# A LayerNorm's scale: computed on both halves of the partitions, spread by a matmul into PSUM

## The chip, the cores and the metric

The kernel runs on one core of one Trainium2 chip. Its engines work side by side, each with its own queue: TensorE (PE in the profile), VectorE (DVE), ScalarE (ACT), GpSimd (POOL) and SyncE (SP), which here issues the DMAs. SBUF and PSUM have 128 partitions. What counts is the device time of one execution in microseconds (us), the median of several runs.

## The reference

Two layers over 1024 tokens of 1024 channels, in float32. Each layer has a mixer (attention and short convolution, or pooling and latent attention) and a convolutional FFN, and behind each of the two stands a LayerNorm over the channels of a token:

```
def layer_norm(x, g, b):
    x32 = x.astype(jnp.float32)
    mu = jnp.mean(x32, axis=-1, keepdims=True)
    var = jnp.mean(jnp.square(x32 - mu), axis=-1, keepdims=True)
    y = (x32 - mu) * lax.rsqrt(var + LN_EPS)
    return (y * g + b)

x = layer_norm(DN_ALPHA * x + (1.0 + g_m) * y, ln_mix_g[l], ln_mix_b[l])
h = x * (1.0 + sc_f) + sh_f
y = conv_ffn(h, ffn_w_up[l], ffn_conv_w[l], ffn_w_down[l])
x = layer_norm(DN_ALPHA * x + (1.0 + g_f) * y, ln_ffn_g[l], ln_ffn_b[l])
```

The four norms of the two layers are what the change touches.

## The kernel before

Activations lie with channels on the partitions and tokens on the columns: eight tiles `r[0..7]` of 128 channels by 512 tokens hold one half of the tokens. Matrix products run in three passes over split operands (`mm3`: high by high, high by low, low by high; L289 to L291), where `split` (L267 on ScalarE, L268 on VectorE or GpSimd) makes a high and a low part.

A norm (class `Norm`) goes over one half of the tokens at a time. `gated` (L495, VectorE) adds a product from PSUM to the residual; `add` (L505, GpSimd) sums the eight tiles of `r` into `ln_acc`. `mean` multiplies that sum by a 128x128 tile of 1/1024 on TensorE (L515), so that every partition gets the mean of its column's token, subtracts it from the eight tiles on VectorE (L529; L521 in the last part), squares them on ScalarE and sums the squares into two tiles `ln_sq` (L536). `var` does the same with the squares (L545, PSUM, 128 identical rows), takes the root on ScalarE (L549) and the reciprocal on VectorE (L550) over all 512 columns, and multiplies the eight tiles of `r` by it (L556), VectorE with both operands in SBUF. For each tile ScalarE then makes the norm's output `xo` (L563), which SyncE stores, and GpSimd the next layer's input `h` (L572, named `r` where it is made in place, which then waits for `xo`), whose split into `h_f` feeds the next products.

TensorE's program order is written by hand. The code issues its matmuls in the order of the text, and `mean` and `var` are put off by `defer`: a running sum of estimated TensorE time (`spend`) says after which product `tick` issues them. TensorE executes in that order and doesn't overtake. The orders of VectorE, ScalarE, GpSimd and SyncE are set by a scheduler that simulates the program; `tc.high_priority` moves an instruction ahead of others that are ready.

`var` runs at nine places. N1 and N2: layer 0's mixer norm, first and second half of the tokens. N1 falls among the output projection's products (`oproj`, around 630 us), N2 among the first FFN products (`up`, around 684 us). N3 and N4: layer 0's FFN norm, among the last products of `dn` (1409 us) and among layer 1's first products (`lat`, 1447 us). N5 and N6 (1840 and 1893 us): layer 1's mixer norm, as N1 and N2. N7 to N9: the last norm, whose first half (N7, 2573 us) falls among the last `dn` products, while the second half goes in two parts of 256 columns (N8, 2592 us, and N9, 2599 us); in these two, GpSimd makes ten of the sixteen multiplications of L556. In the last part (`end`) the eight tiles of squares go to TensorE one by one, without being summed before.

In the FFN, `plain` multiplies by weights that are loaded and split on the way (`whi_up` on ScalarE; `wlo_up` on VectorE for the first half of the tokens, on GpSimd for the second); `activate` makes the three taps of the convolution (`cv`, L703, VectorE).

Of the kernel before, what the change touches and what calls it, by code (L numbers as in the profile page):

```python
# [10 lines left out]
F32 = mybir.dt.float32  # L11
# [3 lines left out]
AF = mybir.ActivationFunctionType  # L15
ALU = mybir.AluOpType
# [3 lines left out]
P = 128  # L20
D = 1024
# [8 lines left out]
LN_EPS = 1e-5  # L30
# [177 lines left out]
def trunk(ctx, tc, t, out):  # L208
    nc = tc.nc
    V, A, G, T = nc.vector, nc.scalar, nc.gpsimd, nc.tensor  # L210

    def pool(name, bufs=1, side="left", space=None):
        if space is not None:
            return tc.tile_pool(name=name, bufs=bufs, space=space, reuse_waits="tile")
        return tc.tile_pool(name=name, bufs=bufs, side=side, reuse_waits="tile")

    cpool = ctx.enter_context(pool("const"))
# [10 lines left out]
    def spend(us):  # L228
        clock[0] += us
# [13 lines left out]
    def load(dst, src, eng=None):  # L243
        (eng or nc.sync).dma_start(dst, src)
# [14 lines left out]
    def bank_aux(name):  # L259
        return aux[0].tile([P, HALF], F32, tag="aux", name=name)  # L260

    def half(hf):
        return slice(hf * HALF, (hf + 1) * HALF)

    def split(hi, lo, src, lo_eng="dve"):

        A.copy(hi, src)  # L267
        (V if lo_eng == "dve" else G).tensor_tensor(lo, src, hi.bitcast(F32), ALU.subtract)  # L268
# [42 lines left out]
    A.activation(cond, cT, AF.Silu)  # L311
    eps_ln = cpool.tile([P, 1], F32, name="eps_ln")
    V.memset(eps_ln, LN_EPS)
    eps_rms = cpool.tile([P, 1], F32, name="eps_rms")
    V.memset(eps_rms, RMS_EPS)

# [89 lines left out]
    class Stream:  # L406
# [12 lines left out]
        def open_norm(self, e):  # L419
            self.tmp = self.n.enter_context(pool(f"ln{e}_{self.name}", bufs=2, side="right"))  # L420
            self.ones = self.tmp.tile([P, P], F32, tag="ones", name="ones_d", bufs=1)
            V.memset(self.ones, 1.0 / D)

        def open_rows(self):

            self.rows = self.n.enter_context(pool(f"rows_{self.name}", side="right"))
            self.left = {F32: [], F32R: []}
            self.order = ["u0", "rawg", "cond", "u0", "mod_raw", "rawg", "u1", "u1"]
# [30 lines left out]
    class Norm:  # L459
# [79 lines left out]

        def var(self):  # L540
            r, f, hf = self.r, self.f, self.hf
            var = bank_aux("ln_var")[:, : self.c.stop - self.c.start]
            n = len(self.sq)
            for e in range(n):
                T.matmul(var, lhsT=self.st.ones, rhs=self.sq[e], start=e == 0, stop=e == n - 1)  # L545
            spend(1.7)
            rstd = self.tile("acc", "rstd")
            with tc.high_priority(offset=2 * AHEAD):
                A.activation(rstd, var, AF.Sqrt, bias=eps_ln)  # L549
                V.reciprocal(rstd, rstd)  # L550

            pooled = ()
            if rstd.shape[-1] < HALF:
                pooled = (3, 5) if self.end else PAIRED
            for dt in PAIRED:
                (G if dt in pooled else V).tensor_tensor(r[dt], r[dt], rstd, ALU.mult)  # L556
                xo = r[dt] if self.h is None else self.tile("xo", "xo")
                if self.end and dt in (3, 5, 6, 7):
                    (G if dt in pooled else V).tensor_scalar(
                        xo, r[dt], f[:, 0, dt : dt + 1], f[:, 1, dt : dt + 1], ALU.mult, ALU.add  # L560
                    )
                else:
                    A.activation(  # L563
                        xo, r[dt], AF.Identity, bias=f[:, 1, dt : dt + 1],
                        scale=f[:, 0, dt : dt + 1],
                    )
                if self.h is None:
                    load(self.dst[dt, :, half(hf)][:, self.c], xo)
                    continue
                load(xa_dram[hf, dt], xo)  # L570
                h32 = r[dt] if self.keep else self.tile("h32", "h32")
                G.tensor_scalar(  # L572
                    h32, r[dt], f[:, 2, dt : dt + 1], f[:, 3, dt : dt + 1], ALU.mult, ALU.add
                )
                split(self.h.t[hf][:, 0, dt], self.h.t[hf][:, 1, dt], h32)
# [757 lines left out]
    start = ExitStack()  # L1333
# [545 lines left out]
    with ExitStack() as s:  # L1879
# [32 lines left out]
        for hf in range(2):  # L1912
            c = half(hf)
            xs = h.xs(hf)
            for base, n, mi, lo in ((4, 3, 0, 0), (7, 2, 1, 3)):
                z = []
                acc = tmp.tile([P, HALF], F32, tag="zacc", name="zacc", bufs=2)
# [237 lines left out]
def build(nc, arrays):  # L2155
    t = {
        k: nc.dram_tensor(f"in_{k}", v.shape, mybir.dt.from_np(v.dtype), kind="ExternalInput").ap()
        for k, v in arrays.items()
    }
    out = nc.dram_tensor("out_xT", (KD, P, S), F32, kind="ExternalOutput").ap()  # L2160
    with tile.TileContext(nc, schedule_with_timeline_sim=True) as tc:
        trunk(tc, t, out)
# [15 lines left out]
```

## Time and profile before

| | us |
|---|---|
| runs | 2625.12, 2621.45, 2623.29 |
| median | 2623.29 |
| profiled execution | 2616.24 |
| its span | 2614.4 |
| PE, DVE, ACT, POOL busy | 2375.9, 2169.9, 1378.1, 1078.8 |

The profile shows one execution, from the first instruction to the last (the span); the 1.84 us around it belong to the run's time. In its rows `L556` is a line of the kernel, `r<-r,rstd` is output and inputs by the program's names, and `128x512` the shape, partitions by columns. A bracket at the end of a row is the time that the engine stood idle before it, and whose end released it. "PEclk" is the clock granted to TensorE, as a share of its full 2.4 GHz: 0.5 is the lower of its two levels, 1.2 GHz, and a value between is a mean over a stretch with both.

### The profile page before, as it was taken

What the parts mean: (1) busy time and instruction counts of PE and PEld (TensorE: products, weight loads), DVE (VectorE), ACT (ScalarE), POOL (GpSimd) and SP (SyncE); (2) the same over time, 40 slices, a digit from 0 to 9 for tenths busy, and PEclk for the clock granted to TensorE, in tenths of its full rate; (3) what the DMA queues carried; (4) which work ended last, traced back from release to release, by engine and by line L of the source; (5) the groups of instructions that cost most, each with busy time, mean ns of one, the idle gap of its engine ahead of it and who ended that gap; (6) DMA issues with size and microseconds to landing.
All of it is one profiled execution on the core that took longest, in us unless ns stands there. A gap on an engine that the chain in (4) does not pass through costs nothing. (4 is left out here: it accounts for less than half of the span.)

```text
span 2614.4 us, 32451 instructions
## 1 busy us (share of the span) xinstructions
PE 2375.9 (91%) x10762; PEld 1905.7 (73%) x10762; DVE 2169.9 (83%) x3495; ACT 1378.1 (53%) x2449; POOL 1078.8 (41%) x816
## 2 busy tenths in 40 slices
PE   6799997989978988998999898998989999998997
PEld 4678785877656767876787677887666888876786
DVE  7868888886898999988977868786798877788976
ACT  4558734884644344553434547675555555563434
POOL 0000003757663222324537535554675333334536
PEclk9999998999989999999999999999989999999999
DMA  6513320225434555344314331224432322244313
GB/s 249 170 42 108 97 69 17 74 77 163 133 107 159 183 172 162 104 132 151 91 55 130 93 111 39 68 80 151 138 110 93 109 84 82 93 139 140 100 48 107
DMA packets 126473, 289.44 MB, mean 111 GB/s; under 512 B 16032, under 2 KB 23712, under 8 KB 125408
## 3 DMA queue, kind: packets, MB, share of 16 engines
q1 hardware_dynamic: 125152, 283.16, 34.3%
q10 hardware_dynamic: 1152, 4.19, 0.5%
q8 instruction: 85, 1.39, 0.2%
q14 instruction: 84, 0.69, 0.1%
HBM read 234.87 MB, written 48.23 MB: 108 GB/s over the span
## 5 line engine op out<-in xcount | busy, mean ns | idle before, releaser
L703 DVE SCALAR_TENSOR_TENSOR cv<-u,taps,cv 128x512 f32<-128x512 f32 x352 | 308.4, 902 | 18.1 <-ACT cv L701 16.4
L834 POOL TENSOR_TENSOR s<-rawg 128x512 f32<-128x512 f32 (+3 forms) x60 | 78.4, 1307 | 258.8 <-DVE wlo_ups L268 87.1
L268 POOL TENSOR_TENSOR v<-v,v 128x512 fp32r<-128x512 f32 x8 | 11.9, 1492 | 416.9 <-ACT v L267 416.9
L999 DVE SCALAR_TENSOR_TENSOR r<-dn,mod,r 128x512 f32<-128x512 f32 x198 | 147.0, 745 | 41.8 <-PE dn L291 39.8
L701 ACT ACTIVATE cv<-u,taps 128x512 f32<-128x512 f32 x176 | 124.3, 721 | 56.4 <-DMA z<-cv 29.0
L289 PE MATMUL up<-t,wh 128*128 128x512 f32 x288 | 119.3, 414 | 31.5 <-ACT u L873 31.5
L707 ACT ACTIVATE cv<-cv 128x512 f32<-128x512 f32 x88 | 55.6, 632 | 144.4 <-DVE cv L703 143.5
L290 PE MATMUL up<-h_f,whi_up 128*128 128x512 f32 x256 | 105.6, 412 | 25.7 <-DVE h_f L268 25.7
L873 ACT COPY u<-up 128x512 f32<-128x512 f32 x144 | 83.9, 584 | 77.3 <-issue 33.3
L378 DVE CUSTOM_DVE_ANT_0 mod_raw<-mod_raw,cond_row 128x512 f32<-128x512 f32 (+1 forms) x112 | 106.0, 953 | 20.1 <-DMA mod_raw<-in_ada_w 16.1
L268 DVE TENSOR_TENSOR wl<-rawg,wh 128x512 fp32r<-128x512 f32 (+3 forms) x120 | 119.7, 1000 | 2.6 <-ACT wh L267 2.6
L290 PE MATMUL up<-t,wh 128*128 128x512 f32 x288 | 117.9, 409 | 0.0
L291 PE MATMUL up<-t,wl 128*128 128x512 f32 x288 | 117.6, 408 | 0.0
L835 POOL TENSOR_TENSOR s<-s,raw_upv 128x512 f32<-128x512 f32 x36 | 50.5, 1403 | 161.0 <-DMA raw_upv<-in_w_up 138.7
L267 ACT CAST wh<-rawg 128x512 fp32r<-128x512 f32 (+3 forms) x120 | 65.0, 545 | 98.2 <-PE dn L290 51.3
L289 PE MATMUL up<-h_f,whi_upa 128*128 128x512 f32 x288 | 114.5, 398 | 0.8 <-ACT whi_upa L267 0.8
L291 PE MATMUL up<-h_f,wlo_upa 128*128 128x512 f32 x288 | 113.7, 395 | 0.7 <-DVE wlo_upa L268 0.7
L290 PE MATMUL up<-h_f,whi_upa 128*128 128x512 f32 x288 | 113.0, 392 | 0.0
L268 DVE TENSOR_TENSOR pl<-pt,ph 128x128 fp32r<-128x128 f32 (+2 forms) x192 | 99.6, 545 | 14.8 <-ACT ph L267 14.1
L291 PE MATMUL up<-h_f,wlo_up 128*128 128x512 f32 x256 | 104.1, 407 | 6.0 <-POOL wlo_up L268 6.0
L842 POOL TENSOR_TENSOR raw_upv<-raw_upv,s 128x512 f32<-128x512 f32 x36 | 60.3, 1675 | 118.7 <-DVE wlo_upa L268 118.7
L289 PE MATMUL up<-h_f,whi_up 128*128 128x512 f32 x256 | 106.0, 414 | 1.6 <-ACT whi_up L267 0.8
(755 smaller groups left out, 8562.7 us busy)
## 6 DMA issues: line engine op xcount, KB each, us to landing
mod_raw<-in_ada_w SPq DMA_DIRECT2D x96, 256.0 KB, 2.9
z<-cv SPq DMA_DIRECT2D x88, 256.0 KB, 2.0
raw_upv<-in_w_up SPq DMA_DIRECT2D x36, 512.0 KB, 3.7
rawg<-in_w_up SPq DMA_DIRECT2D x34, 512.0 KB, 3.7
raw_up<-in_w_up SPq DMA_DIRECT2D x32, 512.0 KB, 3.7
z<-z SPq DMA_DIRECT2D x56, 256.0 KB, 2.7
xa_dram<-xo SPq DMA_DIRECT2D x48, 256.0 KB, 2.3
raw_dr<-in_w_dr SPq DMA_DIRECT2D x32, 384.0 KB, 3.1
```

The source lines that it names most:

```text
L267: A.copy(hi, src)
L268: (V if lo_eng == "dve" else G).tensor_tensor(lo, src, hi.bitcast(F32), ALU.subtract)
L289: T.matmul(ps, lhsT=wh, rhs=xh, start=start, stop=False, skip_group_check=more)
L290: T.matmul(ps, lhsT=wh, rhs=xl, start=False, stop=False, skip_group_check=more)
L291: T.matmul(ps, lhsT=wl, rhs=xh, start=False, stop=stop, skip_group_check=more)
L378: V.tensor_tensor_reduce(out=raw, in0=raw, in1=self.cond[:, o], scale=1.0, scalar=0.0, op0=ALU.mult, op1=ALU.add, accum_out=self.acc[:, j, ...
L701: A.activation(y[n], u[:, 0:HALF], AF.Copy, scale=self.taps[:, c, 0:1])
L703: V.scalar_tensor_tensor(y[n], u[:, k : k + HALF], self.taps[:, c, k : k + 1], y[n], ALU.mult, ALU.add,)
L834: G.tensor_tensor(s1, g[:, c0], g[:, c1], ALU.add)
L842: G.tensor_tensor(v[:, c1], v[:, c1], s2, ALU.subtract)
L873: A.copy(dst, ps)
L999: V.scalar_tensor_tensor(r, ps, self.gate[:, dt : dt + 1], r, ALU.mult, ALU.add)
```

## The change

The variance matmuls put the first half of the columns on partitions 0 to 63 and the second half on 64 to 127: for each of the two groups of columns, the same sum with only 64 columns of the tile of ones. Root and reciprocal then work on half as many columns. A selector `spread` of 64 equal rows (1/1024, zero elsewhere) brings each group back to all 128 partitions by a matmul into a PSUM bank; the factor 4/1024 under the root makes up for the sum over 64 equal rows. All multiplications of `r` read the scale from PSUM, which GpSimd doesn't do here; so those that it made in the tail are VectorE's.

```diff
+    eps_row = cpool.tile([P, 1], F32, name="eps_row")
+    V.memset(eps_row, LN_EPS * 4 / D)
...
+            self.spread = self.tmp.tile([P, 2, P], F32, tag="spread", name="spread", bufs=1)
+            for g in range(2):
+                for r_ in range(2):
+                    V.memset(self.spread[64 * r_ : 64 * r_ + 64, g], 1.0 / D if g == r_ else 0.0)
...
         def var(self):
             r, f, hf = self.r, self.f, self.hf
-            var = bank_aux("ln_var")[:, : self.c.stop - self.c.start]
+
+            q = (self.c.stop - self.c.start) // 2
+            var = bank_aux("ln_var")[:, :q]
             n = len(self.sq)
-            for e in range(n):
-                T.matmul(var, lhsT=self.st.ones, rhs=self.sq[e], start=e == 0, stop=e == n - 1)
+            for g in range(2):
+                for e in range(n):
+                    T.matmul(
+                        var[64 * g : 64 * g + 64], lhsT=self.st.ones[:, :64],
+                        rhs=self.sq[e][:, g * q : g * q + q], start=e == 0, stop=e == n - 1,
+                    )
             spend(1.7)
-            rstd = self.tile("acc", "rstd")
+            rs = self.tile("acc", "rstd")[:, :q]
             with tc.high_priority(offset=2 * AHEAD):
-                A.activation(rstd, var, AF.Sqrt, bias=eps_ln)
-                V.reciprocal(rstd, rstd)
+
+                A.activation(rs, var, AF.Sqrt, bias=eps_row, scale=4.0 / D)
+                V.reciprocal(rs, rs)
+            rstd = bank_aux("rstd")[:, : 2 * q]
+            for g in range(2):
+                T.matmul(
+                    rstd[:, g * q : g * q + q], lhsT=self.st.spread[:, g], rhs=rs, start=True,
+                    stop=True,
+                )
+            spend(1.2)
...
-                (G if dt in pooled else V).tensor_tensor(r[dt], r[dt], rstd, ALU.mult)
+                V.tensor_tensor(r[dt], r[dt], rstd, ALU.mult)
```

TensorE's queue around N1, among the products of the output projection's second half (`y` is the mixer's output), before:

```order
L291 MATMUL oproj<-y_5527,wlo_w_evo_2_5639 128x512
L545 MATMUL ln_var<-ln_sq,ones_d 128x512 x2
L289 MATMUL oproj<-y_5506,whi_w_evo_3_5745 128x512
L290 MATMUL oproj<-y_5506,whi_w_evo_3_5745 128x512
L291 MATMUL oproj<-y_5506,wlo_w_evo_3_5746 128x512
```

and of the change:

```order
L291 MATMUL oproj<-y_5534,wlo_w_evo_2_5646 128x512
L555 MATMUL ln_var<-ln_sq,ones_d 64x256 x4
L567 MATMUL rstd<-rstd,spread 128x256 x2
L289 MATMUL oproj<-y_5513,whi_w_evo_3_5757 128x512
L290 MATMUL oproj<-y_5513,whi_w_evo_3_5757 128x512
L291 MATMUL oproj<-y_5513,wlo_w_evo_3_5758 128x512
```

Two matmuls have become four, and two more, which read the reciprocal's result, stand between them and the next product. It is so at all nine places.

VectorE's queue at N2, from the reciprocal on (`h_f` is the split of the next input, eight in all; `cv` the convolution of the first half's tokens), before:

```order
L550 RECIPROCAL rstd<-rstd 128x512
L703 SCALAR_TENSOR_TENSOR cv<-u,taps_5935,cv 128x512
L556 TENSOR_TENSOR r<-r,rstd 128x512 x8
L742 COPY u<-halo_5955 128x2
L268 TENSOR_TENSOR wlo_up_0_3_6297<-raw_up_0_3_6294,whi_up_0_3_6296 128x1024
L745 COPY halo_5955<-u 128x2
L775 TENSOR_TENSOR t_6379<-r,blk 128x512
L703 SCALAR_TENSOR_TENSOR cv<-u,taps_5935,cv 128x512
L268 TENSOR_TENSOR h_f_1_5290<-r,h_f_1_5290 128x512 x2
L268 TENSOR_TENSOR wlo_up_0_25_6328<-raw_up_0_25_6325,whi_up_0_25_6327 128x1024
L745 COPY halo_5955<-u 128x2
L703 SCALAR_TENSOR_TENSOR cv<-u,taps_5935,cv 128x512
```

and of the change:

```order
L564 RECIPROCAL rstd<-rstd 128x256
L724 SCALAR_TENSOR_TENSOR cv<-u,taps_5947,cv 128x512
L763 COPY u<-halo_5967 128x2
L577 TENSOR_TENSOR r<-r,rstd 128x512 x8
L796 TENSOR_TENSOR t_6396<-r,blk 128x512
L268 TENSOR_TENSOR h_f_1_5292<-r,h_f_1_5292 128x512 x3
L797 TENSOR_TENSOR r<-r 128x512
L268 TENSOR_TENSOR h_f_1_5292<-r,h_f_1_5292 128x512
L796 TENSOR_TENSOR t_6411<-r,blk 128x512
L268 TENSOR_TENSOR wlo_up_0_3_6314<-raw_up_0_3_6311,whi_up_0_3_6313 128x1024
L798 TENSOR_TENSOR r<-r,t_6396 128x512
L766 COPY halo_5967<-u 128x2
```

Four splits `h_f` stand in this piece instead of two, and up to the eighth three fewer `cv` do.

GpSimd's queue at the same place (`r<-r,fm` makes `h` in place; `wlo_up_1_0` is the second half's first weight; `blk` and `t` are sums and splits for later products), before:

```order
L572 TENSOR_SCALAR r<-r,fm_5280 128x512 x4
L772 TENSOR_TENSOR blk<-h_f_0_5289 128x512
L572 TENSOR_SCALAR r<-r,fm_5280 128x512 x2
L268 TENSOR_TENSOR wlo_up_1_0_6438<-raw_up_1_0_6435,whi_up_1_0_6437 128x1024
L773 TENSOR_TENSOR blk<-h_f_0_5289 128x512
L572 TENSOR_SCALAR r<-r,fm_5280 128x512
L778 TENSOR_TENSOR blk<-blk,r 128x512
L572 TENSOR_SCALAR r<-r,fm_5280 128x512
L268 TENSOR_TENSOR wlo_up_1_22_6469<-raw_up_1_22_6466,whi_up_1_22_6468 128x1024
L778 TENSOR_TENSOR blk<-blk,r 128x512
```

and of the change, up to that weight:

```order
L593 TENSOR_SCALAR r<-r,fm_5282 128x512
L799 TENSOR_TENSOR blk<-blk,r 128x512
L593 TENSOR_SCALAR r<-r,fm_5282 128x512
L799 TENSOR_TENSOR blk<-blk,r 128x512
L593 TENSOR_SCALAR r<-r,fm_5282 128x512
L268 TENSOR_TENSOR t_5957<-blk,t_5957 128x512
L793 TENSOR_TENSOR blk<-h_f_0_5291 128x512
L268 TENSOR_TENSOR t_5958<-blk,t_5958 128x512
L794 TENSOR_TENSOR blk<-h_f_0_5291 128x512
L793 TENSOR_TENSOR blk<-h_f_0_5291 128x512
L268 TENSOR_TENSOR wlo_up_1_0_6455<-raw_up_1_0_6452,whi_up_1_0_6454 128x1024
L268 TENSOR_TENSOR wlo_up_1_22_6486<-raw_up_1_22_6483,whi_up_1_22_6485 128x1024
```

The second half's first two weights have moved behind the last rows of `h` and five more operations.

VectorE's queue at N8 and N9, the end of the program, before:

```order
L495 SCALAR_TENSOR_TENSOR r<-dn,mod_85,r 128x256
L550 RECIPROCAL rstd<-rstd 128x256
L495 SCALAR_TENSOR_TENSOR r<-dn,mod_85,r 128x256
L505 TENSOR_TENSOR ln_acc<-ln_acc,r 128x256
L521 TENSOR_TENSOR r<-r,ln_mean 128x256 x8
L550 RECIPROCAL rstd<-rstd 128x256
L556 TENSOR_TENSOR r<-r,rstd 128x256 x6
L559 TENSOR_SCALAR r<-r,last 128x256 x2
```

and of the change:

```order
L502 SCALAR_TENSOR_TENSOR r<-dn,mod_87,r 128x256 x3
L564 RECIPROCAL rstd<-rstd 128x128
L577 TENSOR_TENSOR r<-r,rstd 128x256 x8
L502 SCALAR_TENSOR_TENSOR r<-dn,mod_87,r 128x256
L512 TENSOR_TENSOR ln_acc<-ln_acc,r 128x256
L528 TENSOR_TENSOR r<-r,ln_mean 128x256 x8
L564 RECIPROCAL rstd<-rstd 128x128
L577 TENSOR_TENSOR r<-r,rstd 128x256 x8
L580 TENSOR_SCALAR r<-r,last 128x256 x2
```

N8's eight multiplications, GpSimd's before, stand between its reciprocal and the last residual and sum, and ahead of N9's subtractions.

## Rows read from the trace of the kernel before

**Rows 1.** The page's first part: engine, busy us, share of the span, instructions.
```profile
PE 2375.9 (91%) x10762; PEld 1905.7 (73%) x10762; DVE 2169.9 (83%) x3495; ACT 1378.1 (53%) x2449; POOL 1078.8 (41%) x816
```

**Rows 2.** Timeline at N1 and N2: start, us, engine, line, operation, [idle before].
```profile
630.08 1.12 PE L545 MATMUL ln_var<-ln_sq,ones_d 128*128 128x512 f32 x2 [1.82 <-POOL ln_sq L536]
...
631.24 0.69 ACT L549 ACTIVATE rstd<-ln_var,eps_ln 128x512 f32<-128x512 f32 x1 [1.27 <-PE ln_var L545]
...
631.97 3.35 DVE L550 RECIPROCAL rstd<-rstd 128x512 f32<-128x512 f32 x1 [4.89 <-ACT rstd L549]
...
683.76 2.35 PE L545 MATMUL ln_var<-ln_sq,ones_d 128*128 128x512 f32 x4 [0.44 <-DVE ln_sq L536]
...
688.80 0.69 ACT L549 ACTIVATE rstd<-ln_var,eps_ln 128x512 f32<-128x512 f32 x1
```

**Rows 3.** Timeline of VectorE at N1, N3 and N4.
```profile
635.36 5.74 DVE L556 TENSOR_TENSOR r<-r,rstd 128x512 f32<-128x512 f32 x8
...
1416.72 8.31 DVE L556 TENSOR_TENSOR r<-r,rstd 128x512 f32<-128x512 f32 x8
...
1433.74 4.86 DVE L529 TENSOR_TENSOR r<-r,ln_mean 128x512 f32<-128x512 f32 x8
```

**Rows 4.** Single lines: shortest/median/longest ns, first and last start, shapes.
```profile
L550 DVE RECIPROCAL rstd<-rstd x9: 1753/3353/3354, 632.0 to 2604.3; 128x512 f32<-128x512 f32 x7, 128x256 f32<-128x256 f32 x2
...
L529 DVE TENSOR_TENSOR r<-r,ln_mean x64: 402/680/689, 616.0 to 2587.0; 128x512 f32<-128x512 f32 x56, 128x256 f32<-128x256 f32 x8
```

**Rows 5.** VectorE's groups by line and shape: busy us, mean ns, idle before.
```profile
L556 DVE TENSOR_TENSOR r<-r,rstd 128x512 f32<-128x512 f32 x56 | 44.4, 860 | 0.1
...
L529 DVE TENSOR_TENSOR r<-r,ln_mean 128x512 f32<-128x512 f32 x56 | 34.1, 681 | 4.3 <-PE ln_mean L515 4.1
```

**Rows 6.** Timeline of GpSimd behind N1, N2 and N6.
```profile
650.32 0.78 POOL L572 TENSOR_SCALAR h<-r,fm 128x512 f32<-128x512 f32 x1
...
695.00 4.15 POOL L572 TENSOR_SCALAR r<-r,fm 128x512 f32<-128x512 f32 x2 [10.07 <-ACT xo L563]
...
1900.94 6.33 POOL L572 TENSOR_SCALAR r<-r,fm 128x512 f32<-128x512 f32 x2 [9.69 <-ACT xo L563]
```

**Rows 7.** Timeline of PE: its long waits behind N1 to N6.
```profile
669.45 1.21 PE L515 MATMUL ln_mean<-ln_acc,ones_d 128*128 128x512 f32 x2 [3.90 <-POOL ln_acc L505]
...
731.05 0.80 PE L290 MATMUL up<-h_f,whi_up 128*128 128x512 f32 x1 [10.94 <-DVE h_f L268]
...
1426.34 0.49 PE L290 MATMUL lat<-h_f,whi_lat 128*128 128x512 f32 x1 [2.62 <-DVE h_f L268]
...
1492.49 0.80 PE L289 MATMUL pool<-pdh,whi_pool 128*128 128x512 f32 x1 [5.32 <-ACT pdh L267]
...
1937.68 0.79 PE L290 MATMUL up<-h_f,whi_up 128*128 128x512 f32 x1 [10.81 <-DVE h_f L268]
```

**Rows 8.** Windows: us, busy PE, PEld, DVE, ACT, POOL, PEclk, DMA, GB/s.
```profile
670.00:672.00 2.00, 2.00 (x6) 1.44 (x5) 1.31 (x3) 0.59 (x1) 0.00 (x0) 0.59 0.04 14
672.00:674.00 2.00, 2.00 (x6) 1.55 (x6) 2.00 (x4) 1.84 (x4) 0.09 (x1) 0.56 0.04 8
...
705.00:720.00 15.00, 13.70 (x59) 10.47 (x57) 15.00 (x16) 12.76 (x19) 15.00 (x8) 1.00 0.50 159
```

**Rows 9.** The chain that ended last, in the tail: start, us, what.
```profile
2572.61 1.72 PE ln_var L545 x4
...
2580.75 0.43 PE ln_mean L515 x2
...
2598.73 4.99 PE ln_var L545 x14
...
2606.04 3.35 DVE r L556 x6
```

**Rows 10.** Timelines of GpSimd and VectorE at N8 and N9.
```profile
2595.21 5.71 POOL L556 TENSOR_TENSOR r<-r,rstd 128x256 f32<-128x256 f32 x8 [1.63 <-DVE rstd L550]
...
2597.01 2.74 DVE L521 TENSOR_TENSOR r<-r,ln_mean 128x256 f32<-128x256 f32 x8 [0.79 <-PE ln_mean L515]
```

## The prediction

> **What bounds the kernel now.** I read first the page's busy shares, then the timelines around each of the nine places where a norm's scale is made, then the sources of single lines, then PE's waits, and last the chain of waits over the tail. PE is busy for 91% of the span and VectorE for 83% [rows 1], so both matter, and which of them ends a wait has to be read place by place. N1 and N2 below are the two halves of layer 0's mixer norm, N3 and N4 of its FFN norm, N5 and N6 of layer 1's mixer norm, N7 the first half of the last norm, N8 and N9 the two 256-column parts of its second half.
>
> At N1 the reader is to see the chain that the change rebuilds [rows 2]: the last variance matmul at 630.08, the root at 631.24 (0.69 us), the reciprocal at 631.97 (3.35 us). PE takes no part in what follows: its next matmuls are products that need nothing of the norm. Eight multiplications of r by the scale come next, 5.74 us of VectorE here and 8.31 us at N3, while the eight subtractions of the mean, of the same shape but with one operand in PSUM, take 4.86 us at N4 [rows 3]. Over the program 56 multiplications take 860 ns on average and 56 subtractions 681 ns [rows 5], and no subtraction took more than 689 ns [rows 4]. Meanwhile GpSimd, which scales the same rows right behind, has two of its 512-column operations spread over 4.15 us at N2 and 6.33 us at N6; alone one takes 0.78 us [rows 6]. So a multiplication with both operands in SBUF and a GpSimd operation stand in each other's way, and one with an operand in PSUM does not show it.
>
> The Trainium skill (page "SBUF — State Buffer", section "Who interferes with whom") says the same: a VectorE instruction with two SBUF inputs and a GpSimd instruction that reads SBUF lock each other out for whole instructions, and one SBUF input avoids that. The trace agrees, with 689 ns as the longest subtraction. The lines below use only the rows.
>
> PE's long waits near the nine places are 3.90 us for N2's mean (released by GpSimd's row sums), 10.94 us before the second half's first `up` products (released by VectorE's split of N2's rows), 10.81 us at the same spot of layer 1, 2.62 and 5.32 us after N3 and N4 [rows 7]. In the tail the chain of waits is PE's products and the norm itself, without such cover [rows 9].
>
> **The change part by part.** The sum is made against the profiled execution, 2616.24 us (span 2614.4 and 1.84 around it). The median of the runs is 2623.29, 7.05 us above it, so the forecast is that median plus the sum.
>
> *Root and reciprocal on half the columns.* The reciprocal of 256 columns is in the trace: 1.75 against 3.35 us [rows 4], 1.60 us less at seven places. The step per column gives, as an estimate, 0.95 us for 128 columns, 0.80 us less at N8 and N9. The root gives 0.2 us.
>
> *Variance matmuls.* Four of 256 columns for two of 512 are the same columns. But the second group of columns needs the first sum of squares again, so three matmuls instead of one or two stand behind the last sum of squares: one more of 0.43 us [rows 9], 0.25 to 0.43 us.
>
> *Spread matmuls.* Two of 256 columns, 0.43 us each at full clock [rows 9]: 0.86 us, 1.1 with the start. So the scale arrives 1.8 us earlier and is then held up by 1.1 to 1.5: a gain of 0.3 to 0.5 us only.
>
> *PE's order.* The spread stands in PE's order right behind the variance, and PE doesn't overtake. Everything behind (the output projection at N1, `up` at N2, `dn` at N3, `lat` at N4) now waits for root and reciprocal: 0.5 + 1.75 + gaps + 0.9, some 3.3 to 3.6 us at N1, N4, N5 and N7; 5.4 at N2, where the root starts 2.7 us behind the last matmul [rows 2], and as much at N6; between the two, 4.4, at N3. This wait is new at all nine places, some 33 us of PE in sum, and whether it costs is a question of the waits behind it.
>
> *r times scale.* With the scale in PSUM I take 4.86 us for eight: 0.9 us less at N1, 3.45 at N3 [rows 3]. GpSimd's pair behind it takes 1.6 us instead of 4.15 to 6.33 [rows 6]. No GpSimd row of before has an operand in PSUM, and the change gives it none: in the tail ten multiplications go to VectorE: eight at N8, two at N9, 0.34 us each (2.74 us for eight subtractions of 256 columns) [rows 10].
>
> *Memsets* for the selector: four of 64x128, each time a norm's scratch is opened, long before its first spread: nothing; if they fell into a VectorE chain, they would cost less than one multiplication. The scale now holds one of the two auxiliary banks until the last multiplication; the next user of that bank comes over 8 us later outside the tail: nothing.
>
> Sum by places:
>
> A (N1, N2). PE loses 3.5 us at N1 and 5.4 at N2, but waits 3.90 and 10.94 us behind them [rows 7], and both waits are released by GpSimd and VectorE. Those get faster: N1 0.4 + 0.9, of which I take 1.1 into N2's mean; at N2 0.4, and 2.6 from GpSimd's unlocked pair. Together −4.1. What is late next: GpSimd's split of the second half's weights has moved behind five more of its operations, some 8 us, about what its eight rows save. I take −4, from −9 (all pairs unlocked) to +3 (weights late).
>
> B (N5, N6). The same, with GpSimd's first pair at 6.33 instead of 4.15 us [rows 6]: −1.1 −0.4 −3.5, so −5, from −10 to +3.
>
> C (N3, N4). PE stalls 4.4 + 3.3, of which the 2.62 wait takes a part, and 1.6 to 3.6 us arrive at `lat`. VectorE's side loses 0.4 + 3.45 at N3 and less at N4: 4 to 6 us earlier. The 5.32 wait behind both hangs on both. I take −2, from −5 to +3.4.
>
> D (N7 to N9). No cover. N7: stall 3.6, one more variance matmul 0.4, restart 0.3 (an estimate): +4.3. N8: eight multiplications, 2.74 us, now stand on VectorE ahead of the last residual, the last sum and so of N9's mean: +2.8 with spread against the shorter reciprocal. N9's mean thus comes 7.1 us late. Then: squares no longer interleaved with N8's outputs on ScalarE −1.5; the second column group's eight matmuls behind the last square +2.0 (before, matmuls follow squares one by one [rows 9]); root and reciprocal −0.9; spread +0.6; eight multiplications unlocked against six in 3.35 us [rows 9, 10], where GpSimd's took 5.71 us for eight: −0.6. Together +6.7, from +3 to +9.
>
> A + B + C + D = −4 − 5 − 2 + 6.7 = −4.3. On the median: 2623.29 − 4.3 = 2619.0.
>
> A fall of TensorE's clock is in no term. After the 3.90 us wait the granted clock was 0.59 and 0.56 over 670 to 674 [rows 8], half speed, which costs 1.7 us of products; after the 2.62 wait it stayed full. In A and B such a fall lies under the next wait.
>
> The Trainium skill (page "TensorE: Matmul & The Clock Gate", Part 1) warns of pauses between bursts of matmuls for this reason, and so speaks against a wait put into PE's order nine times. The trace agrees at the 3.90 us wait. With one fall at each of N3, N4 and N7 the sum would be 5.1 us higher, +0.8.
>
> **Rivals.** *The unlocked GpSimd and VectorE carry all they gain* (20%). For it: the 10.94 and 10.81 us waits are ended by them alone [rows 7]. Against it: VectorE has `cv` work queued between, and is busy for 15.00 of the 15 us ahead of the wait at 731 [rows 8]. A −9, B −10, C −4, D +6.7: −16, so 2607.
>
> *PE's order decides* (25%). Its place is N3, N4 and N7: VectorE's rest of the queue sets when the last split comes at the two fronts, so A and B give 0. At N3 and N4 the new waits, 7.7 us, less the 2.62 us that was waited anyway and the 1.6 us of shorter reciprocal leave +3.4; D +6.7: +10, so 2633. It decides once the fronts give less than 10 us. For it: VectorE without a gap ahead of that wait [rows 8]. Against it: its order there has three `cv` fewer ahead of the last split.
>
> *The change doesn't do what it says*: excluded, since the short reciprocal and the PSUM operand are both in the trace at their price [rows 4].
>
> **How the numbers follow.** Forecast 55%, at 2619.0, its own range 2613 to 2625 (fronts −14 to −4 around −9). Rivals 20% at 2607 and 25% at 2633. The range 2607 to 2634 holds the forecast, half of the first rival and most of the second: 8 in 10. A measurement of this kernel tells 0.2%, 5.2 us, from no change: faster is below 2618.0, slower above 2628.5. Of the forecast's 55 some 24 lie below 2618.0 and 31 above; the first rival adds 20 to faster; the second gives 1 to same and 24 to slower. Faster 0.44, same 0.32, slower 0.24.
>
> **What would show it.** Reciprocals of 1.75 us at seven places; multiplications at 0.68 us with no long ones, and GpSimd's scaling at 0.8 us. PE waits of 3.3 to 5.4 us before `rstd` at nine places. Layer 0's wait at 731 and layer 1's at 1937.7 should end some 4 and 9 us earlier (the second with A's and C's part), and N9's mean some 7 us later relative to the first `dn` products of the tail. I'm wrong in A and B if the waits before `up` end no earlier, and in D if N9's mean is not late or the tail's products fill the wait; a granted clock of half in the stretches behind N3, N4 or N7 would show the dearer case.

## The result, and the profile after

The changed kernel takes 2636.52 us (median of 4 runs, 2634.87 to 2638.45) against 2622.37 (4 runs of before, 2620.92 to 2625.12): slower by 0.53%, ratio 1.0053, 95% interval 1.0036 to 1.0070. The forecast was 2619.0, its range 2607 to 2634. The profiled execution takes 2634.87 us, 18.63 more than that of before.

Everything that the change does for itself is there. The page's first line and three lines by source (shortest/median/longest ns, first and last start, shapes), of the kernel after:

```profile
PE 2393.5 (91%) x10846; PEld 1935.0 (73%) x10846; DVE 2142.6 (81%) x3522; ACT 1377.6 (52%) x2449; POOL 1050.3 (40%) x806
```
```profile
L564 DVE RECIPROCAL rstd<-rstd x9: 952/1753/1753, 634.7 to 2623.7; 128x256 f32<-128x256 f32 x7, 128x128 f32<-128x128 f32 x2
...
L577 DVE TENSOR_TENSOR r<-r,rstd x72: 411/678/689, 638.6 to 2627.8; 128x512 f32<-128x512 f32 x56, 128x256 f32<-128x256 f32 x16
...
L567 PE MATMUL rstd<-rstd,spread x36: 275/634/796, 636.5 to 2625.1; 128*128 128x256 f32 x28, 128*128 128x128 f32 x8
```

The reciprocal takes 1753 and 952 ns as worked out, no multiplication takes more than 689 ns, and VectorE is busy for 27 us less, GpSimd for 28.5 us less than in [rows 1]. What is off is the third line: a pass of the spread takes 634 ns at the median, and a spread needs four. TensorE waits and runs slowly around them. Its timeline after, at N1, N2, the two fronts (the second half's first `up` products, behind N2 and N6) and N7 (in brackets the idle time before, and what ended it):

```profile
632.17 1.98 PE L555 MATMUL ln_var<-ln_sq,ones_d 128*64 128x256 f32 x6 [2.29 <-POOL ln_sq L543]
...
636.50 2.08 PE L567 MATMUL rstd<-rstd,spread 128*128 128x256 f32 x4 [2.35 <-DVE rstd L564]
...
693.20 2.07 PE L567 MATMUL rstd<-rstd,spread 128*128 128x256 f32 x4 [4.67 <-DVE rstd L564]
...
732.31 0.80 PE L291 MATMUL up<-h_f,wlo_up 128*128 128x512 f32 x1 [8.32 <-POOL wlo_up L268]
...
1944.36 0.80 PE L291 MATMUL up<-h_f,wlo_up 128*128 128x512 f32 x1 [8.49 <-POOL wlo_up L268]
...
2584.22 1.85 PE L555 MATMUL ln_var<-ln_sq,ones_d 128*64 128x256 f32 x6 [3.01 <-POOL ln_sq L543]
...
2588.42 2.08 PE L567 MATMUL rstd<-rstd,spread 128*128 128x256 f32 x4 [2.35 <-DVE rstd L564]
```

Three things are to be seen. The waits for the reciprocal are there (2.35 and 4.67 us). At the two fronts the waits of 10.94 and 10.81 us for VectorE's split of N2's and N6's rows [rows 7] are gone, and in their place stand 8.32 and 8.49 us for GpSimd's split of a weight. And at N7 a wait of 3.01 us for GpSimd's sum of squares has come up that [rows 9] does not have. Windows of the stretch behind N7, after (columns as in [rows 8], the granted clock third from the end):

```profile
2584.00:2588.00 4.00, 1.85 (x6) 0.66 (x6) 1.38 (x1) 0.47 (x1) 3.02 (x5) 0.55 0.00 0
2588.00:2590.00 2.00, 1.58 (x5) 1.31 (x5) 0.37 (x1) 0.00 (x0) 0.00 (x0) 0.50 0.00 0
2590.00:2592.00 2.00, 2.00 (x10) 1.91 (x9) 1.46 (x3) 0.74 (x2) 0.00 (x0) 0.50 0.00 0
2592.00:2594.00 2.00, 2.00 (x11) 2.00 (x11) 2.00 (x4) 2.00 (x4) 0.00 (x0) 0.50 0.51 193
```

Two waits with little work between them, and TensorE runs at half speed until 2594: 10 and 11 products in 2 us, where constsel (below) has 19 behind its spread.

To see where the time went, the same matmul was looked up in the traces and its start compared with that in the trace of before. The gain or loss over four stretches (given by the times of before: A 600 to 800, C 1300 to 1500, B 1800 to 2000, D 2535 to the end; the prediction's places), in us, for every kernel that was run:

| kernel | A | C | B | D | sum | by the ratio |
|---|---|---|---|---|---|---|
| forecast | −4 | −2 | −5 | +6.7 | −4.3 | |
| the change | +2.6 | −1.4 | +4.4 | +10.5 | +16.1 | +13.9 |
| fronts | +2.9 | −0.5 | +5.0 | +4.4 | +11.8 | +8.1 |
| tail | +0.3 | +2.5 | −0.1 | +10.1 | +12.8 | +7.3 |
| own | +3.2 | −2.0 | +0.8 | +9.7 | +11.7 | +8.9 |
| deferred | −0.2 | −2.5 | +1.1 | +10.5 | +8.9 | +3.9 |
| n7 | +0.2 | +0.8 | −1.2 | +6.5 | +6.3 | +3.4 |
| n7warm | +1.7 | −0.1 | −1.4 | +5.7 | +5.9 | +2.6 |
| n7defer | +0.9 | +0.4 | −1.6 | +10.5 | +10.2 | +7.6 |
| inert | +0.1 | +0.4 | −1.5 | +4.2 | +3.2 | +1.6 |
| constsel | +2.5 | −2.7 | +4.6 | +3.8 | +8.2 | +8.1 |
| defconst | +0.2 | −3.2 | +0.3 | +0.7 | −2.0 | −3.9 |
| psumrecip | −2.9 | −4.5 | −3.0 | −0.9 | −11.3 | −13.6 |
| psum7 | −3.0 | −4.4 | −5.0 | −1.2 | −13.6 | −14.4 |

The last column is the ratio to the runs of before beside it, times 2622 us; its interval is about 3 us to either side. The sum lies up to 5.5 us above it; the profiled execution of before is one of its shorter ones, and that of tail one of its longer ones. It is one trace each, and up to 2.5 us of A, B or C are the spread between executions: in tail, inert and the three n7 kernels, whose code before 2535 is that of before but for four memsets at each of three places, A, C and B lie between −1.6 and +2.5. D is finer: psumrecip and defconst, with D's code of before, have −0.9 and +0.7. Where a loss "at 731" or "behind N7" is given below, it is measured in the same way, from the start of the stretch to the matmul that runs there in before.

### The profile page after: what moved, and what is told of

It reads as the page before. It is cut to its first block, busy times and chain, and to the rows that moved or that the text cites. A ratio compares the mean times of both kernels' runs of the same rounds, so it can differ in the third digit from the quotient of the medians.

```text
span 2633.1 us, 32646 instructions
## 1 busy us (share of the span) xinstructions
PE 2393.5 (91%) x10846; PEld 1935.0 (73%) x10846; DVE 2142.6 (81%) x3522; ACT 1377.6 (52%) x2449; POOL 1050.3 (40%) x806
## 4 chain that ended last, share of the span: by engine, by line
PE 58%; DVE 19%; DMA 8%; ACT 5%; issue 5%; POOL 5%; SPq 0%; DVEq 0%; ACTq 0%; POOLq 0%
PE up L289 7%; PE up L291 7%; PE up L290 7%; PE dn L289 4%; PE dn L291 4%; PE dn L290 4%; DMA mod_raw<-in_ada_w 3%; DVE cv L724 3%; DVE mod_raw L380 2%; PE pt L1219 1%; DVE t L268 1%; PE yps L1256 1%; DVE wl L268 1%; PE oproj L290 1%; PE oproj L289 1%
## 5 line engine op out<-in xcount | busy, mean ns | idle before, releaser
L268 POOL TENSOR_TENSOR v<-v,v 128x512 fp32r<-128x512 f32 x8 | 11.8, 1480 | 418.3 <-ACT v L267 418.3
L289 PE MATMUL up<-h_f,whi_up 128*128 128x512 f32 x256 | 105.9, 414 | 2.7 <-ACT whi_up L267 2.7
L892 DVE TENSOR_TENSOR u<-up,u 128x512 f32<-128x512 f32 x108 | 73.7, 683 | 39.6 <-PE up L291 39.5
```

Source lines behind the costliest of these rows:

```text
L289: T.matmul(ps, lhsT=wh, rhs=xh, start=start, stop=False, skip_group_check=more)
L892: V.tensor_tensor(dst, ps, dst, ALU.add)
```

## The experiments

**fronts.** The change at N1 to N6 alone, **tail** at N7 to N9 alone.

```diff
+            (self.var_new if self.h is not None else self.var_old)()   # fronts
+            (self.var_new if self.h is None else self.var_old)()       # tail
```

> The change at N1 to N6 alone, the last norm (N7 to N9) as before. From the two traces, matmul for matmul, the stretches of N1 to N6 cost 8 us of the 18.6 and the tail 10. Both theories: 8 us slower than before (2630). If the tail's loss came from before (a later start, another order), it would show here: 12 or more.

> The change at N7 to N9 alone. If the losses add up: 10 us slower than before (2632), with a wait of some 3 us for GpSimd's sum of squares, a wait for the reciprocal of 2.4 us and half clock behind it at N7. If the last norm loses only because it comes late from the fronts: under 4 us.

Measured: fronts 1.0031 (1.0019 to 1.0043), tail 1.0028 (1.0017 to 1.0039), 8.1 and 7.3 us; together 15.4 against the change's 13.9, so the losses add up within their intervals. fronts meets its 8 us, but not for the reason expected: 4.4 us of its loss lie in D, where its code of the norm is that of before. tail's 7.3 lie between its two cases. The reason in D is a row that the change has too. Timeline of PE in fronts:

```profile
2588.27 1.80 PE L606 MATMUL ln_var<-ln_sq,ones_d 128*128 128x512 f32 x2 [3.18 <-POOL ln_sq L543]
```

So N7's wait for the sum of squares does not come from the new way to make the scale. Both kernels carry what causes it, and their sum counts it twice.

**inert** asks what else it can come from: before, with the selector made and not used.

```diff
+            self.spread = self.tmp.tile([P, 2, P], F32, tag="spread", name="spread", bufs=1)
+            for g in range(2):
+                for r_ in range(2):
+                    V.memset(self.spread[64 * r_ : 64 * r_ + 64, g], 1.0 / D if g == r_ else 0.0)
```

> The kernel before with the change's selector made and not used: the four memsets at each of the four places where a norm's scratch is opened, and the constant under the root. In GpSimd's queue the only difference from before is that two sums of squares of N7 stand behind three splits of the last weights. If these memsets alone cause the wait of 3 us for the sum of squares at N7 and the half clock behind it: 3 to 5 us slower than before, all of it behind 2570 us. If the order follows from the norm's own new work: no change.

Measured: 1.0006 (0.9995 to 1.0016), so between 1.3 us faster and 4.2 slower, by which no loss can be told from none; in the trace D is 4.2 us longer. GpSimd's queue in the last norm, before, and in inert (`raw_dr` are the last weights, `ln_sq` the second sum of squares; its last two additions are shown):

```
L536 TENSOR_TENSOR ln_sq<-ln_sq,sq 128x512
L268 TENSOR_TENSOR h_f_1_15775<-raw_dr_6_1_21730,h_f_1_15775 128x512
L268 TENSOR_TENSOR h_f_1_15775<-raw_dr_6_1_21730,h_f_1_15775 128x256
L505 TENSOR_TENSOR ln_acc<-ln_acc,r 128x256
L536 TENSOR_TENSOR ln_sq<-ln_sq,sq 128x512
L268 TENSOR_TENSOR t_16449<-raw_dr_7_1_21736,t_16449 128x512
L268 TENSOR_TENSOR h_f_1_15775<-raw_dr_7_1_21736,h_f_1_15775 128x256
```
```
L268 TENSOR_TENSOR h_f_1_15787<-raw_dr_6_1_21747,h_f_1_15787 128x512
L268 TENSOR_TENSOR h_f_1_15787<-raw_dr_6_1_21747,h_f_1_15787 128x256
L543 TENSOR_TENSOR ln_sq<-ln_sq,sq 128x512
L512 TENSOR_TENSOR ln_acc<-ln_acc,r 128x256
L268 TENSOR_TENSOR t_16466<-raw_dr_7_1_21753,t_16466 128x512
L268 TENSOR_TENSOR h_f_1_15787<-raw_dr_7_1_21753,h_f_1_15787 128x256
L543 TENSOR_TENSOR ln_sq<-ln_sq,sq 128x512
```

Timeline of PE in inert, and its windows there:

```profile
2581.01 1.80 PE L552 MATMUL ln_var<-ln_sq,ones_d 128*128 128x512 f32 x2 [3.19 <-POOL ln_sq L543]
```
```profile
2579.00:2581.00 2.00, 0.00 (x0) 0.00 (x0) 0.00 (x0) 0.00 (x0) 2.00 (x4) 1.00 0.00 0
2581.00:2583.00 2.00, 1.99 (x4) 1.02 (x5) 0.00 (x0) 0.15 (x1) 1.84 (x3) 0.58 0.04 8
```

The memsets fall into VectorE's queue just ahead of N7's subtractions, the scheduler then orders GpSimd's queue otherwise, and TensorE waits for it and slows down: 4.2 us from an edit that the prediction put at nothing. That is shown in the trace; in the times it is not resolved by this run alone. The wait stands in every kernel of the table that makes the selector inside the norm (in n7warm it is filled), and in none of the others.

**constsel**: the whole change, with the selector made once in the constants.

```diff
-            self.spread = self.tmp.tile([P, 2, P], F32, tag="spread", name="spread", bufs=1)
+    spread = cpool.tile([P, 2, P], F32, name="spread")
```

> The change in full, with the selector made once at the start of the program instead of four times. The wait for the second sum of squares at N7 (3.0 us) goes, the one for the reciprocal stays. If the memsets cost what fronts shows in the tail (4.5 us against before with N7 to N9 untouched): 4 us faster than the change, some 10 us slower than before. If not: as the change, 14 us slower than before.

Measured: 1.0031 (1.0020 to 1.0043), 5.8 us less than the change's 13.9, though the intervals of the two ratios overlap. In the traces D goes from +10.5 to +3.8, and A, B and C stay within the spread. At N7 the wait for the squares is gone, that for the reciprocal stays, and alone it does not take the clock down here. Timeline and windows:

```profile
2590.52 1.13 PE L566 MATMUL rstd<-rstd,spread 128*128 128x256 f32 x4 [2.35 <-DVE rstd L563]
```
```profile
2588.00:2590.00 2.00, 0.17 (x1) 0.00 (x0) 1.29 (x1) 0.47 (x1) 1.92 (x4) 1.00 0.00 0
2590.00:2592.00 2.00, 1.48 (x9) 1.38 (x10) 0.78 (x2) 0.00 (x0) 1.84 (x3) 1.00 0.00 0
2592.00:2594.00 2.00, 2.00 (x19) 2.00 (x19) 2.00 (x4) 1.59 (x3) 0.02 (x1) 1.00 0.00 0
```

**n7, n7warm, n7defer** split N7: the change there alone; with seven matmuls more in the waits; with the spread 34 products later.

```diff
+                    if g == 0 and e == 1:
+                        warm(4)                              # n7warm; T.matmul(rstd, ones, sq[0])
+            warm(3)                                          # n7warm, ahead of the spread
+            defer(3.3, lambda: self.scaled(rs, q))           # n7defer, in place of the spread
```

> The change at N7 alone; N8 and N9 with their multiplications on GpSimd, and the six others, as before. From the traces N7 carries 9 of the tail's 10 us: 5 to 9 us slower than before. If instead N8 and N9 carry the tail's loss (the prediction had 4.3 at N7, 2.4 behind it): 3 to 4 us.

> As n7, with seven matmuls more whose result is not used: four ahead of the variance's second sum of squares and three ahead of the spread, where PE waits in n7. They fill the waits, and the waits end as in n7. If the half clock behind the waits costs: granted clock 1.00 throughout, the spread 0.9 us instead of 2.1, the products behind it at 0.12 us, 3 us faster than n7. If only the waits cost: as n7, or up to 1 us slower.

> As n7, with the spread 3.3 us of estimated TensorE time later in PE's order, behind 34 products. No wait for the reciprocal; the wait for the second sum of squares stays (3 us in the change) if GpSimd's order keeps it late. If the place in PE's order is what costs: within 3 us of before, half clock only behind the sum of squares. If N7's multiplications on VectorE come too late for N8: as n7.

Measured: 1.0013 (1.0004 to 1.0022), 1.0010 (1.0002 to 1.0019), 1.0029 (1.0018 to 1.0040). By the ratio, n7's 3.4 us fall in its second case; by the trace N7 carries 6.5 of tail's 10.1 us. All three carry the four memsets. Behind N7 the loss is 3.9 us in inert, 7.4 in n7, 6.0 in n7warm and 9.9 in the change, and 3.3 in constsel, which has the wait for the reciprocal alone; so some 4 us of n7's are inert's and the rest are that wait and its clock. In n7warm the clock stays full and the spread takes half the time; rows of n7 and of n7warm:

```profile
2581.74 1.21 PE L558 MATMUL ln_var<-ln_sq,ones_d 128*64 128x256 f32 x6 [3.02 <-POOL ln_sq L543]
...
2585.31 2.08 PE L570 MATMUL rstd<-rstd,spread 128*128 128x256 f32 x4 [2.35 <-DVE rstd L567]
```
```profile
2578.09 2.84 PE L560 MATMUL rstd<-ln_sq,ones_d 128*128 128x512 f32 x6
...
2580.77 1.03 PE L578 MATMUL rstd<-rstd,spread 128*128 128x256 f32 x4
```

It wins 1.4 us behind N7 and 0.8 in D, not the 3 expected (the ratios don't tell them apart): the waits are the larger part of N7's price, the clock the smaller, though the three filling matmuls end some 0.3 us later than the reciprocal does. n7defer is 4 us slower than n7. Behind N7 it loses 3.5 us, no more than inert, so there the place in PE's order is what costs. But its last multiplications stand among N8's squares, N8's outputs and sums shift, and N9's mean waits for the last sum:

```profile
2605.75 1.19 PE L522 MATMUL ln_mean<-ln_acc,ones_d 128*128 128x256 f32 x2 [4.79 <-DVE ln_acc L512]
```

Its expectations of "within 3 us" and "as n7" were both wrong; here, where little work is left, the later scale cost more than the wait.

**own** tests whether the late weight makes the loss of the fronts.

```diff
+                                    raw = tmp.tile([P, 1024], F32, tag=f"raw{n}", name="raw_own", bufs=1)
+                                    hi = tmp.tile([P, 1024], F32R, tag="whi", name="whi_own", bufs=1)
+                                    lo = tmp.tile([P, 1024], F32R, tag="wlo", name="wlo_own", bufs=1)
```

> The change in full; the second half's first weight of the plain FFN gets buffers of its own (and the second one a load buffer), so that its split no longer stands behind the operations that moved ahead of it. Theory 1, the late weight sets the fronts' loss: PE's waits of 8.3 and 8.5 us for wlo_up go to under 1, and the run is 9 to 12 us faster than the change (2625 to 2628). Theory 2, the wait for the reciprocal and the half clock behind it set the loss at each place: at most 2 us faster than the change (2635).

Measured: 1.0034 (1.0021 to 1.0046), 5 us faster than the change (the intervals overlap), between the two theories. B falls from +4.4 to +0.8, A does not fall. Timeline of PE in own at layer 0's front:

```profile
737.48 0.50 PE L291 MATMUL up<-h_f,wlo_own 128*128 128x512 f32 x1 [2.41 <-POOL wlo_own L268]
...
759.43 0.79 PE L289 MATMUL up<-h_f,whi_up 128*128 128x512 f32 x1 [4.77 <-ACT whi_up L267]
...
762.64 0.79 PE L291 MATMUL up<-h_f,wlo_up 128*128 128x512 f32 x1 [1.99 <-POOL wlo_up L268]
```

The first weight is no longer waited for; in place of the 8.32 us stand 2.41 for the second, and 22 us on the products wait 4.77 us for a later weight (0.81 there before). At 731 own is 2.1 us ahead of before, where the change is 4.9 behind; at 757 own is 7.7 behind, since the next weights are late. In B it is 3.0 ahead at 1937.7, where the change is 7.2 behind. So the late weight makes the loss at the two waits, and the weights behind it take back what its cure gives, all of it in A and part in B.

**deferred**: the change, with the spread of N1 to N6 later in PE's order; **defconst** the same with the selector made once and N7 to N9 as before.

```diff
+            if self.h is not None:
+                defer(3.3, lambda: self.scaled(rs, q))
```

> The change in full, but at N1 to N6 the spread matmuls and what reads them stand 3.3 us of estimated TensorE time later in PE's order, so that products fill the time of root and reciprocal. Theory 1 and 2 together: no wait for the reciprocal, no fall of the clock and the weights in the old order, so only the tail's 10 us stay, less what the shorter work at the fronts gives (the prediction had 9 there): 2623 to 2632. If the spread's lateness costs the fronts what it saves: 2635 as the change.

> The change at N1 to N6 alone, with the spread 3.3 us of estimated TensorE time later in PE's order, the selector made once at the start, and N7 to N9 as before. Everything that was found to cost is out; what stays is the shorter root and reciprocal and the multiplications from PSUM. If the half-width reciprocal is worth its 1.6 us on the path beside what psumrecip has: 13 to 18 us faster than before. If the later spread gives it back (the scale then comes 3 us later than in psumrecip): 6 to 13 us faster.

Measured: deferred 1.0015 (1.0006 to 1.0025), defconst 0.9985 (0.9975 to 0.9996). No wait for the reciprocal (but 0.50 us at N3), the second half's first weight at its old place behind six rows of `h`, A and B at about nothing instead of +2.6 and +4.4. deferred's interval lies wholly below the change's. So the place of the spread in TensorE's queue did cost what the fronts lost. But the 9 us that the prediction had there are not won. Timeline of PE in deferred:

```profile
727.85 0.79 PE L290 MATMUL up<-h_f,whi_up 128*128 128x512 f32 x1 [5.73 <-DVE h_f L268]
...
757.76 0.50 PE L289 MATMUL up<-h_f,whi_up 128*128 128x512 f32 x1 [2.17 <-ACT whi_up L267]
```

The front ends 3.2 us earlier than in before (731.05) though it starts 1.8 later, and the gain is given back at the next weights: 5.0 us at 731, 0.2 at 800. defconst's 3.9 us miss both of its expected ranges.

**psumrecip** is the kernel before with one edit: the reciprocal of all 512 columns is written into a PSUM bank. **psum7** does so at N7 too.

```diff
-                V.reciprocal(rstd, rstd)
+                if self.h is not None:
+                    sd, rstd = rstd, bank_aux("rstd")
+                    V.reciprocal(rstd, sd)
```

> The kernel before with one edit: at N1 to N6 the reciprocal of all 512 columns is written into a PSUM bank, so that the multiplications of r read the scale from PSUM and PE has no part in it. Multiplications at 0.68 us, GpSimd's scaling at 0.8 us, no new waits on PE, GpSimd's weights in the old order. If the unlocked multiplications are worth what the prediction said (9 us at the two fronts, 2 at N3 and N4): 8 to 11 us faster than before. If the stretch behind each front takes it back, as in own and deferred (4 to 5 us won by 731, gone by 800): within 3 us of before.

> As psumrecip, with N7's reciprocal in PSUM too. N7's multiplications are alone on the two engines already (5.27 us for eight against 4.87), so 0 to 1 us faster than psumrecip: 13 to 15 us faster than before. If the bank that it holds delays a mean of N8: up to 2 us slower than psumrecip.

Measured: psumrecip 0.9948 (0.9936 to 0.9960), 2610.89 us, 13.6 us faster than before (10.5 to 16.8), more than the 8 to 11 expected; psum7 0.9945 (0.9929 to 0.9961), 2609.45 us. Both beat both kernels. Rows of psumrecip: the reciprocal by source, the multiplications by shape (busy us, mean ns), GpSimd and PE at N2:

```profile
L552 DVE RECIPROCAL rstd<-rstd x6: 3360/3361/3361, 634.3 to 1890.0; 128x512 f32<-128x512 f32 x6
```
```profile
L560 DVE TENSOR_TENSOR r<-r,rstd 128x512 f32<-128x512 f32 x56 | 34.5, 686 | 0.1
```
```profile
693.86 1.55 POOL L576 TENSOR_SCALAR r<-r,fm 128x512 f32<-128x512 f32 x2 [9.71 <-ACT xo L567]
...
706.69 2.83 POOL L268 TENSOR_TENSOR wlo_up<-raw_up,whi_up 128x1024 fp32r<-128x1024 f32 x1
```
```profile
729.04 0.79 PE L290 MATMUL up<-h_f,whi_up 128*128 128x512 f32 x1 [10.48 <-DVE h_f L268]
```

The long reciprocal costs 8 ns more into PSUM (3361 against 3353 [rows 4]). GpSimd's pair takes 1.55 us instead of 4.15 [rows 6], its queue at N2 keeps the order of before row for row, and A, B and C are shorter (D within the spread).

## Why the prediction was wrong

The direction was wrong. The gains were of about the right size in sum and the costs were not. The rival that was slower, "PE's order decides" (2633), was 3.5 us short, but that is luck: it put the loss at N3 and N4, where C is −1.4, and none at the fronts, where A and B lost 7.0.

*What bounds the kernel.* Right: multiplications with both operands in SBUF and GpSimd's operations hold each other up, and one operand in PSUM ends that for the multiplications. psumrecip isolates it: −10.4 us over A, B and C, where the forecast had −11 for the three, with the shorter reciprocal and the stalls at N3 and N4 included. By places they differ (−2.9, −3.0 and −4.5 in A, B and C against −4, −5 and −2), so that the sums meet is in part luck. Of the half-width reciprocal's own 1.6 us, 0.3 to 0.5 was forecast to be left behind the spread; no run shows it: defconst has it and is 9.7 us behind psumrecip, but its scale is also put off.

*Spread, 0.86 to 1.1 us.* Mis-sized: 2.07 to 2.08 us at half clock at N1 to N7 except N4, while N4 (1.13), constsel (1.13) and n7warm (1.03) give the forecast price at full clock. No term had a fall of the clock; behind each of N1 to N7 at least one window of 2 us has 0.50. N7's share of it is small (n7warm, 1.4 us); at the fronts it was not measured apart from the wait. N4 after, where the clock falls only behind the spread:

```profile
1456.60 1.13 PE L567 MATMUL rstd<-rstd,spread 128*128 128x256 f32 x4 [2.37 <-DVE rstd L564]
```
```profile
1458.00:1460.00 2.00, 2.00 (x6) 1.55 (x5) 2.00 (x4) 1.69 (x3) 1.44 (x2) 0.50 0.00 0
```

*PE's order, A and B.* The waits were right (2.35 to 4.74 us each at N1 to N7, 1.45 and 1.46 at N8 and N9), and so was the claim that the long waits behind cover them: N1's loss of 6.6 us is 0.1 behind N2's mean (at 672), and own, with the same waits, is ahead of before at 731. "GpSimd's split of the second half's weights has moved behind five more of its operations, some 8 us, about what its eight rows save" is the step that failed. The last split of VectorE did end earlier, at 728.39 (731 before), but the weight came 19 us later. Its first rows were as fast as forecast (the first pair 1.52 us), but all eight, summed over its timeline, take 13.5 us where before they took 15.9: 2.3 us saved, not 8. The five operations take 10.0 us, 1.83 of them a wait for VectorE. And the weight had stood ahead of the last two rows, which the step did not count. Rows of GpSimd and VectorE after:

```profile
696.95 1.52 POOL L593 TENSOR_SCALAR r<-r,fm 128x512 f32<-128x512 f32 x2 [9.56 <-ACT xo L584]
...
718.27 1.21 POOL L593 TENSOR_SCALAR r<-r,fm 128x512 f32<-128x512 f32 x1
...
729.47 5.56 POOL L268 TENSOR_TENSOR wlo_up<-raw_up,whi_up 128x1024 fp32r<-128x1024 f32 x2
```
```profile
726.64 1.75 DVE L268 TENSOR_TENSOR h_f<-r,h_f 128x512 fp32r<-128x512 f32 x1
```

In before that split ran at 710.57 for 2.88 us, with the last row of `h` behind it:

```profile
710.57 2.88 POOL L268 TENSOR_TENSOR wlo_up<-raw_up,whi_up 128x1024 fp32r<-128x1024 f32 x1
...
718.53 1.71 POOL L572 TENSOR_SCALAR r<-r,fm 128x512 f32<-128x512 f32 x1
```

And the weight is needed by the first products of the second half, while the split that was late before was needed only by later ones: before, 19 of the 24 products on this weight were done when the wait of 10.94 us began; after, two were, and 22 stood behind the weight. Of the forecast's A and B, −4 and −5, the change made +2.6 and +4.4. That deferred and defconst keep the weight at its old place and lose A's and B's cost shows that the wait in PE's order brought the reordering with it; by which buffer the scheduler came to it was not tried. The forecast's bound of +3 for late weights was near A and short of B. A second step failed beside it: what is won at the front's wait was taken as won, and in own and deferred the next weights take it back.

*C.* Right in sign and size, as far as one trace tells: −1.4 against −2, and −4.5 without the waits of PE (psumrecip).

*D, +6.7.* Two errors. The memsets, "nothing", cost 4.2 us alone (inert) and 6.7 in the change (+10.5 against constsel's +3.8), through GpSimd's order, and with them went a fall of the clock that the single wait of 2.35 us does not bring at N7 of constsel. What was worked out was too dear, +6.7 where constsel has +3.8: +3.3 behind N7 against +4.3, +2.3 from there to N9's mean against +2.8, and −1.8 at the end against −0.4. The restart of 0.3 us in the sum came from no row, and no run shows it by itself. Of the terms, the chain of waits after shows eight multiplications of 2.74 us as forecast, the variance of N9 5.13 us against 4.99 [rows 9], where +2.0 and −1.5 had been put down:

```profile
2612.70 2.74 DVE r L577 x8
...
2618.14 5.13 PE ln_var L555 x32
...
2623.70 0.96 DVE rstd L564
```

*The clock as a warning.* The Trainium skill (page "TensorE: Matmul & The Clock Gate", Part 1) was weighed, at 0.8 us slower than the median of before, and left out of the sum. The rows after agree with its warning, and for several short waits too: half clock at N1, N2 and N7, where the waits are 2.3 to 4.7 us. It told the direction; most of the size lay elsewhere.

Still open: how the loss of 7.0 us at the fronts (A and B) divides between the wait itself, the half clock and the reordered weights (without the first weight's lateness the whole run is 5 us faster), and why deferred's early fronts are caught by the next weights where psumrecip's are not.

## What to carry to other kernels

A scale that VectorE makes and then reads many times can go straight into PSUM: here that cost 8 ns a reciprocal, took one of VectorE's two operands off SBUF beside a busy GpSimd, and was worth 13.6 us. A step that sends a short chain through TensorE in the middle of its queue has to be priced as a stop of TensorE, with the clock behind it. Where a scheduler sets the queues, compare the order of every engine at every place with a tight wait, also for edits that seem idle: four memsets on VectorE moved two sums on GpSimd, and the last stretch became 4.2 us longer.

## What the runs showed of the hardware

VectorE writes a 128x512 reciprocal into PSUM in 3361 ns, into SBUF in 3353. Two waits of TensorE, of 3.0 and then 2.35 us, with 1.2 to 1.9 us of matmuls between took the granted clock from 1.00 to 0.50, for some ten us in the change and seven in n7. A single wait of 2.35 us did not at N7 of constsel; one of 2.37 us at N4 of the change did for some 3 us, and one of 3.19 us in inert as well. Matmuls without use in the waits kept it at 1.00 (n7warm). VectorE's multiplications of 128x512 took 860 ns on average with both operands in SBUF beside GpSimd's work [rows 5], and 686 with one of them in PSUM (psumrecip).
